# Four projections of a decoder block: output copies and search counts in program order, the forget gates beside the fifth projection

## The chip, the cores and the metric

One core of one Trainium2 chip runs the whole kernel in one launch. The metric is the device time in microseconds (us) of one execution; three executions of the kernel before took 1204.28, 1204.99 and 1205.78 us, so the time before is their median, 1204.99 us.

## The reference, cut to what matters

A decoder layer on 1024 tokens of width 1024. The input is normalised and goes through one combined projection, whose columns feed two groups of attention heads:

```python
proj = h @ w_in
(aq, ak, av, iq, ik, iw, bq, bk, bv, bf) = split(proj)
# group A: each query attends to its 256 best keys by an indexer's score
score = einsum('bqh,bqhs->bqs', iw, relu(einsum('bqhd,bsd->bqhs', iq, ik)))
_, idx = top_k(where(causal, score, -inf), 256)
# group B: a running sum of log forget gates is added to the logits
log_f = log_sigmoid(bf + b_forget)
cum = cumsum(log_f, axis=1)
logits = q @ k.T * scale + cum_q - cum_k
```

Both groups are normalised, go through an output projection, and a mixture of 32 experts follows. Nothing of that later part is touched here.

## The kernel before, in words

**Stages.** The kernel loads and normalises x, projects the indexer's keys and queries and makes the scores (`index_scores`), projects the values (`v_tile`), then projects the queries and keys of both groups, then runs sixteen attention heads as one software pipeline (n = 0 to 16), then output projection and experts. All tensors are float32; each projection is done in three passes of a high and a low part (`PASSES`), so one block of 512 output columns takes 8 x 3 = 24 matmuls (`proj_T`).

**The projection stage.** A loop over z = 0 to 3 projects queries and keys of group B, two blocks of 128 rows each (`proj_pair`, called with m = 0 and 1); after it come `KA` (keys of group A) and `QA` 0 to 3. Each call of `proj_pair` makes two halves of 512 columns. This text numbers the halves 0 to 25: z = 0 has halves 0 to 3, z = 1 has 4 to 7, z = 2 (the fifth and sixth projection) has 8 to 11, z = 3 has 12 to 15, `KA` has 16 and 17, `QA` 0 to 3 have 18 to 25. A half's result lies in one of four PSUM buffers of `ps1`, so half n can start only when the result of half n - 4 has been copied out. Two instructions copy it: `pjh` on ACT rounds it to the high part, then `pjl` on DVE subtracts that from the PSUM result for the low part. When both halves are done, two DMAs of SP store the pair to DRAM (`QB`, `KB`, `KA`, `QA`). Weights come by DMAs of SP too (`load_w`, tiles `wbr` and `waqr`); each 128 x 1024 chunk is split by ACT (high part, `wbh`, `waqh`) and POOL (low part, `wbl`, `waql`). The weights of `QA` 2 and 3 are loaded by `load_aq(1)`, which stands in program order behind `QA` 0, and SP issues its four last DMAs behind the stores of `QA` 0.

**The search.** Beside the projections the 256th best score of each query is found by bisection (`Search`, 33 steps). Each step has two groups of tiles. Group X (tiles 6 and 7) is counted by two ACT instructions (`sign`, tile `sjunk`), whose thresholds come from three small DVE instructions (`halve`, lines 492 to 494: `flag`, `low`, `low`). Group Y (tiles 5, 4, 3, 2) is counted by four DVE instructions (`tally`, 768, 640, 512 and 384 columns) and two small ones (`flip`, `bits`). Step 16 also rewrites the keys of all six tiles on DVE (`lower`). `tick(n)` emits n ticks, two of which are a step (step 16 takes four, so 68 in all): the value projections emit 12, which are steps 0 to 5, and each half of a projection emits 2 behind its copies, except the second halves of `QA` 2 and 3, which emit none; the last 8 are left for the first attention heads.

**The gates.** The forget gates of group B come from `tz`: four long DVE instructions on 8 partitions (lines 614, 617, 618, 621), a scan among them, and five on ACT (615, 616, 620, 622, 623). They depend on each other in turn: DVE `fa`, ACT exp and ln, DVE `fz` and scan, ACT `CU`, DVE `CU`, ACT `CU`. `prep(0)` reads `CU` long after, for the first attention head.

**What sets the order.** A scheduler orders the instructions of each engine by its own model of their times; each engine then runs its list strictly in that order. `ko` (`keep_in_program_order`) takes an instruction out of this choice: all instructions of an engine that have it stay in the order in which the code emits them. `paced` only keeps an instruction from being put ahead of a given matmul. Before, the copies `pjh` and `pjl` are free and the counts are paced.

Of the kernel before, what the change touches and what calls it, by code (L numbers as in the profile page):

```python
# [8 lines left out]
F32 = mybir.dt.float32  # L9
F32R = mybir.dt.float32r  # L10
# [3 lines left out]
AF = mybir.ActivationFunctionType  # L14
OP = mybir.AluOpType
# [3 lines left out]
L = 1024  # L19
# [14 lines left out]
def dap(t, off, ap):  # L34
    return bass.AP(tensor=t.tensor, offset=t.offset + off, ap=ap)
# [3 lines left out]
def hymba_block(ctx: ExitStack, tc: tile.TileContext, x, c, w_ada, b_ada, g_mix, w_in, b_forget,  # L39
# [3 lines left out]
    V, S, G, T, Q = nc.vector, nc.scalar, nc.gpsimd, nc.tensor, nc.sync  # L43
# [37 lines left out]
    def ps1(name, shape=(128, 512), dt=F32):  # L81
        return psum.tile(list(shape), dt, name=name, tag="p", bufs=4)

    def ps2(name, shape=(128, 1024), dt=F32):
        return psum.tile(list(shape), dt, name=name, tag="m", bufs=2)
# [4 lines left out]
    def dump(name, ap):  # L90
        if name in dbg:
            Q.dma_start(dbg[name], ap)
# [136 lines left out]
    p = ps2("pcol")  # L229
    for k in range(NK):  # L230
        column(p, 1, k)
    for j in range(8):
        for q in range(4 if j == 7 else 1):
            sl = slice(q * 256, (q + 1) * 256) if j == 7 else slice(0, 1024)
# [16 lines left out]
    for k in range(NK):  # L251
        hi, lo, t = u(f"hh{k}", F32R), u(f"hl{k}", F32R), u("ht")
# [27 lines left out]
    def proj_T(w, n0, n):  # L280
        p = ps1("pp")
        i = 0
        for k in range(NK):
            for a, b in PASSES:
                at["mm"] = T.matmul(p[:, :n], w(k, a), hT[b][k][:, n0:n0 + n], start=(i == 0), stop=(i == 23))  # L285
                i += 1
        return p
# [13 lines left out]
    for hf in range(2):  # L301
        sl = slice(hf * 512, (hf + 1) * 512)
        p = pk[hf]
# [64 lines left out]
    p = ps1("piw")  # L368
# [214 lines left out]
    def tick(n, mark=None):  # L583
        if mark is not None:
            at["pace"] = mark
        for _ in range(n):
            if next(steps, "end") == "end":
                return
# [3 lines left out]
    def load_b(z):  # L592
        return load_w("wb", [((C_BK if z % 2 else C_BQ) + z // 2 * 256, 256)])

    def load_aq(g):
        return load_w("waq", [(C_AQ + g * 128 + m * 64 + z * 256, 64) for m in range(2) for z in range(2)])

    def load_k():
        g2 = u("g2", shape=(128, 8, 128))
        for j in range(2):  # L600
            Q.dma_start(g2[:, j * 4:j * 4 + 4], dap(w_in, j * 512 * WIN + C_AK, [[WIN, 128], [128 * WIN, 4], [1, 128]]))
        return split(g2, "g2", (128, 8, 128), G), load_aq(0)
# [3 lines left out]
        v_tile(1, wv1, t, lambda: tick(1 + t % 2, at["mm"]))  # L606


    CU = u("CU", F32R)
    if True:  # L610
        R = slice(96, 104)
        z, a1 = u("fz"), u("fa")
        V.tensor_scalar(tz[R], tz[R], bfg[R], None, op0=OP.add)
        V.scalar_tensor_tensor(a1[R], tz[R], -1.0, tz[R], op0=OP.mult, op1=OP.max)
        S.activation(a1[R], a1[R], AF.Exp, scale=-1.0)
        S.activation(a1[R], a1[R], AF.Ln, bias=1.0)
        V.scalar_tensor_tensor(z[R], tz[R], 0.0, a1[R], op0=OP.min, op1=OP.subtract)
        V.tensor_tensor_scan(a1[R], ones[R, 0:1].to_broadcast([8, 1024]), z[R], 0.0, op0=OP.mult, op1=OP.add)
        dump("cum", a1[R])
        S.activation(CU[96:104], a1[R], AF.Copy)  # L620
        V.tensor_sub(CU[64:72], a1[R], CU[R].bitcast(F32))
        S.activation(CU[32:40], CU[R].bitcast(F32), AF.Copy, scale=-1.0)
        S.activation(CU[0:8], CU[64:72].bitcast(F32), AF.Copy, scale=-1.0)


    def proj_pair(w, cols, name, scale, beside=None):

        d = dram.tile([2, 128, L], F32, name=name)
        hi, lo = u("pjh", F32R), u("pjl", F32R)
        for hf in range(2):  # L630
            sl = slice(hf * 512, (hf + 1) * 512)
            p = proj_T(lambda k, a: w(k, a, cols), hf * 512, 512)
            S.activation(hi[:, sl], p, AF.Copy, scale=scale)
            V.scalar_tensor_tensor(lo[:, sl], p, scale, hi[:, sl].bitcast(F32), op0=OP.mult, op1=OP.subtract)  # L634
            if beside is None or not hf:
                tick(PT.pop(0), at["mm"])
            if beside:
                at["pe"] = at["pace"] = at["mm"]
                for f in beside[hf]:
                    f()  # L640
        Q.dma_start(d[0], hi.bitcast(F32))
        Q.dma_start(d[1], lo.bitcast(F32))
        return d

    QB, KB, QA = [None] * 4, [None] * 4, [None] * 4
    PT = [2] * 8 + [2] * 8 + [2] * 8
    for z in range(4):
        w, dst, g = wb, KB if z % 2 else QB, z // 2
        wb = load_b(z + 1) if z < 3 else load_k()
        for m in range(2):  # L650
            dst[g * 2 + m] = proj_pair(w, slice(m * 128, (m + 1) * 128), f"{'QK'[z % 2]}B{g}{m}", 1.0 if z % 2 else 0.125)

# [72 lines left out]
    def fill_k(par, d):  # L725
        cp(kx[par][MAIN[par]], d[0, MAIN[par]])
# [167 lines left out]
    def prep(n):  # L894
# [3 lines left out]
        if n < 8:  # L898
            h = 2 * j + par
            fill_q(par, QB[j])  # L900
            fill_k(par, KB[j])
            cp(qx[par][e + 2:e + 3], CU[96 + h:97 + h], G)
            cp(qx[par][e + 3:e + 4], CU[64 + h:65 + h], G)
            cp(kx[par][e:e + 1], CU[32 + h:33 + h], G)
# [158 lines left out]
    g2s, w = wb  # L1063
    KA = proj_pair(lambda k, a, sl: g2s[a][:, k, sl], slice(0, 128), "KA", 1.0)
    for m in range(4):
        if m == 2:
            rows, finish = max_steps(0)
            rows = [f for _, f in rows]
            beside = [rows[0:3], rows[3:5]]
        elif m == 3:  # L1070
            beside = [rows[5:7], [rows[7], finish]]
        else:
            beside = None
# [3 lines left out]
        if m == 1:  # L1077
            w = w1
            operand_tiles(0)
            prep(0)  # L1080
        if m == 2:
            operand_tiles(1)
            prep(1)
    at["pace"] = at["pe"] = at["mm"]
    after(S.preload_act_table_set("natural_log_exp_and_others"), at["mm"])

    if True:
# [342 lines left out]
    for i in range(NT):  # L1430
# [11 lines left out]
        if i in (5, 7):  # L1442
            i0, n = {5: (0, 4), 7: (4, 2)}[i]
            A, B = tables(n)
            p = count_pairs(i0, n)
# [12 lines left out]
    p = count_pairs(6, 1)  # L1458
# [10 lines left out]
    p = count_pairs(7, 1)  # L1469
# [202 lines left out]
    for e in range(NE):  # L1672
# [34 lines left out]
        else:  # L1707
            bfin = u("bfin")
            for hf in range(2):
                p = ps1("pbf")  # L1710
                for k in range(4):
                    i = 24 + hf * 4 + k
# [41 lines left out]
    with tc.If(most > 128):  # L1754
# [4 lines left out]
        f = u("ovf", shape=(128, 32, 32))  # L1759
# [30 lines left out]
        for i in range(NT):  # L1790
            for c_ in range(2):
                j = i * 2 + c_
                d = G.indirect_dma_start(
                    out=tab2d, out_offset=bass.IndirectOffsetOnAxis(ap=fi[:, 3, j:j + 1], axis=0),
                    in_=ent[:, i, c_], in_offset=None, bounds_check=NO * 128 - 1, oob_is_err=False)
# [30 lines left out]
        for o in range(NO):  # L1826
# [13 lines left out]
            for z in range(2):  # L1840
                for k in range(NK):
# [6 lines left out]
                                   op0=OP.mult, op1=OP.mult)  # L1848
# [50 lines left out]
```

## Time and profile before

| | |
|---|---|
| median of three runs | 1204.99 us |
| the profiled execution | 1199.19 us, its span 1197.2 us |
| PE busy | 1055.7 us (88%) |
| DVE busy | 919.0 us (77%) |
| ACT busy | 670.0 us (56%) |
| POOL busy | 300.3 us (25%) |

The span is the time from the first to the last instruction; 2.0 us lie around it. A row of the timeline is: start, duration, engine, line, operation, tiles, and in square brackets the idle time ahead of it and who ended that. The stage that the change touches runs from 195 to about 360 us of the span.

### The profile page before, as it was taken

To read this page: it belongs to the slowest core of one execution; us is meant where nothing else is said; L and a number is where in the kernel's file an instruction comes from. 1 tells how busy PE (TensorE), PEld (TensorE's weight loads), DVE (VectorE), ACT (ScalarE), POOL (GpSimd) and SP (SyncE) were. 2 spreads that over 40 slices of the span, in tenths; PEclk is the share of its full clock that TensorE was granted. 3 is DMA by queue.
4 is the path that set the end of the run, shared out by engine and by line. 5 is a ranking of instruction groups with operands and counts; after the bars stand their busy time and mean duration, and the time that the engine had idled before them with its cause. 6 is when DMAs were issued, how large, how long until landed. Compare 5 with 4: busy or idle time off the path is not lost.

```text
span 1197.2 us, 15378 instructions
## 1 busy us (share of the span) xinstructions
PE 1055.7 (88%) x4983; PEld 796.5 (67%) x4983; DVE 919.0 (77%) x1785; ACT 670.0 (56%) x1177; POOL 300.3 (25%) x253
## 2 busy tenths in 40 slices
PE   2789999699988998998989999975999999889881
PEld 2678899588865555654656678864777777666650
DVE  5946568899976589566578665795999999888847
ACT  7544666764546545654554622334777777656635
POOL 0341031212040110213212212551222222333223
PEclk9699999899998999999999999986999999999986
DMA  8510102243463433556336634776999999999946
GB/s 345 164 36 1 41 20 65 106 150 114 149 169 89 108 81 81 133 142 195 115 87 198 245 123 141 247 251 216 311 342 320 308 314 308 317 317 315 321 117 247
DMA packets 91414, 219.94 MB, mean 184 GB/s; under 512 B 30516, under 2 KB 40932, under 8 KB 91328
## 3 DMA queue, kind: packets, MB, share of 16 engines
q1 hardware_dynamic: 75776, 185.23, 46.5%
q0 software_dynamic: 15552, 33.66, 10.3%
q8 instruction: 42, 0.69, 0.2%
q14 instruction: 44, 0.36, 0.1%
HBM read 192.43 MB, written 42.99 MB: 197 GB/s over the span
## 4 chain that ended last, share of the span: by engine, by line
PE 49%; DVE 24%; DMA 16%; ACT 5%; issue 3%; SPq 1%; POOL 1%; DVEq 0%; ACTq 0%; POOLq 0%
PE pgu L69 10%; PE py L69 6%; PE pst L69 6%; DVE mjunk L460 6%; PE po L69 6%; PE pout L69 5%; DMA raw<-in_w_gate_dram 4%; DMA raw<-in_w_down_dram 4%; PE pp L285 3%; PE pmax L69 3%; PE pvv L407 2%; DMA qx<-mr 2%; PE pxt L74 2%; ACT sjunk L464 1%; DMA raw<-in_w_up_dram 1%
## 5 line engine op out<-in xcount | busy, mean ns | idle before, releaser
L69 PE MATMUL po<-P,VT 128*128 128x512 f32 (+3 forms) x384 | 148.3, 499 | 0.3 <-ACT P L793 0.3
L793 ACT ACTIVATE P<-pst 128x512 f32<-128x512 f32 x192 | 90.9, 489 | 95.1 <-PE pst L69 93.2
L1570 POOL DMA_INDIRECT x2d<-y,tab x31 | 59.3, 1912 | 204.9 <-DVE wgu1l L1492 46.1
L69 PE MATMUL pst<-qx,kx 128*128 128x512 f32 x192 | 94.3, 491 | 13.3 <-DMA qx<-mr 11.2
L758 DVE TENSOR_REDUCE mx<-pmax 128x1 f32<-128x128 f32 (+3 forms) x80 | 52.7, 674 | 44.6 <-PE pmax L69 44.2
L69 PE MATMUL py<-raw,af 128*128 128x512 f32 x128 | 69.2, 623 | 14.3 <-DMA raw<-in_w_down_dram 14.3
L69 PEld LDWEIGHTS po<-P,VT 128*128 128x128 f32 x384 | 66.1, 195 | 18.0 <-issue 9.8
L69 PE MATMUL pmax<-kx,qx 128*128 128x512 f32 (+1 forms) x192 | 68.1, 420 | 6.4 <-DMA kx<-KB 2.0
L69 PE MATMUL py<-wd0h,ahl 128*128 128x512 f32 x128 | 67.9, 530 | 2.4 <-ACT wd0h L1491 1.9
L69 PE MATMUL pst<-qy,ky 128*128 128x512 f32 x192 | 67.6, 352 | 0.0
L358 DVE SCALAR_TENSOR_TENSOR score<-relu,iw,score 128x384 f32<-128x384 f32 (+5 forms) x42 | 43.1, 1026 | 26.7 <-ACT relu L353 23.7
L69 PEld LDWEIGHTS pst<-qx,kx 128*128 128x128 f32 x192 | 37.9, 197 | 34.2 <-issue 20.8
L285 PE MATMUL pp<-hh,wbh 128*128 128x512 f32 x128 | 51.2, 400 | 9.3 <-DVE pjl L634 9.3
L755 DVE CUSTOM_DVE_ANT_0 mjunk<-pmax,madd 128x384 bf16<-128x384 f32 (+5 forms) x48 | 42.6, 888 | 20.6 <-PE pmax L69 20.5
L69 PE MATMUL pout<-woh,oh 128*128 128x512 f32 x128 | 52.2, 408 | 2.4 <-DVE ssq L871 2.4
L460 DVE TENSOR_SCALAR_CACHE_REDUCE mjunk<-k,low 128x768 bf16<-128x768 uint16 (+1 forms) x64 | 51.8, 810 | 1.5
L1482 POOL DMA_INDIRECT xg<-h2d,tab x32 | 39.0, 1218 | 49.6 <-PE pxt L74 35.2
L1492 DVE TENSOR_TENSOR wgu2l<-raw,wgu2h 128x512 fp32r<-128x512 f32 x64 | 43.8, 685 | 9.7 <-ACT wgu2h L1491 9.6
L285 PE MATMUL pp<-hl,wbh 128*128 128x512 f32 x128 | 50.9, 398 | 0.0
L69 PE MATMUL pout<-woh,ol 128*128 128x512 f32 x128 | 50.8, 397 | 0.0
L285 PE MATMUL pp<-hh,wbl 128*128 128x512 f32 x128 | 50.8, 397 | 0.0
L69 PE MATMUL pout<-wol,oh 128*128 128x512 f32 x128 | 50.4, 394 | 0.0
(430 smaller groups left out, 3263.1 us busy)
## 6 DMA issues: line engine op xcount, KB each, us to landing
raw<-in_w_gate_dram SPq DMA_DIRECT2D x64, 512.0 KB
raw<-in_w_up_dram SPq DMA_DIRECT2D x64, 512.0 KB
raw<-in_w_down_dram SPq DMA_DIRECT2D x64, 512.0 KB
wada<-in_w_ada_dram POOLq DMA_DIRECT2D x32, 512.0 KB, 5.5
x<-in_x_dram SPq DMA_DIRECT2D x16, 512.0 KB
wada<-in_w_ada_dram SPq DMA_DIRECT2D x16, 512.0 KB
wbr<-in_w_in_dram SPq DMA_DIRECT2D x8, 512.0 KB
qy<-QB SPq DMA_DIRECT2D x16, 256.0 KB
```

The costliest lines, as they stand in the source:

```text
L69: i = tc.keep_in_program_order(T.matmul(*a, **k))
L74: i = tc.keep_in_program_order(T.transpose(*a))
L285: at["mm"] = T.matmul(p[:, :n], w(k, a), hT[b][k][:, n0:n0 + n], start=(i == 0), stop=(i == 23))
L358: last = V.scalar_tensor_tensor(score[i], r, wv, score[i], op0=OP.mult, op1=OP.add)
L407: at["mm"] = T.matmul(p[:, :ng], hT[a][k][:, t * 128:(t + 1) * 128], parts[k // kk][b][:, k % kk, :], start=(i == 0), stop=(i == 23))
L460: paced(V.tensor_scalar(mjunk[:, :(i + 1) * 128], src, thr, None, op0=op, op1=OP.add, accum_out=self.col(self.cnt, i)))
L755: V.tensor_tensor_reduce(mjunk[:, :w_], p[:, :w_], madd[i], 1.0, NEG, OP.add, OP.max, accum_out=mx[0][:, i:i + 1])
L758: V.tensor_reduce(mx[0][:, i:i + 1], p[:, :w_], AX.X, OP.max)
L793: S.activation(P[hf, kb][0], p[:, :m], AF.Exp)
L1482: return ko(G.indirect_dma_start(out=XG[e], out_offset=None, in_=h2d, in_offset=bass.IndirectOffsetOnAxis(ap=tab[:, e:e + 1], axis=0), bou ...
L1492: ko(V.tensor_tensor(lo, w, hi.bitcast(F32), op=OP.subtract))
L1570: return G.indirect_dma_start(out=x2d, out_offset=bass.IndirectOffsetOnAxis(ap=at_, axis=0), in_=y, in_offset=None, bounds_check=L - 1, oo ...
```

## The change

Three things. The copies `pjh` and `pjl` get `ko`. While `at["pin"]` is true, from the loop over z to the end of the projections, `paced` gives `ko` to every count of the search too (and to the other paced instructions of that stretch); so the copies and the counts of an engine stand in the order of the code: copies of half n, then that half's step of the search, then the copies of half n + 1. And the gates become a function `gates()`, which is called at z = 2, between the loads for z = 3 and the fifth projection, and no longer ahead of the loop. `pinned` is defined and not used. `proj_pair` moves above the gates.

```diff
     def paced(i):
+        if at.get("pin"):
+            ko(i)
         return after(i, at["pace"]) if "pace" in at else i
...
-    CU = u("CU", F32R)
-    if True:
...
-            S.activation(hi[:, sl], p, AF.Copy, scale=scale)
-            V.scalar_tensor_tensor(lo[:, sl], p, scale, hi[:, sl].bitcast(F32), op0=OP.mult, op1=OP.subtract)
+            ko(S.activation(hi[:, sl], p, AF.Copy, scale=scale))
+            ko(V.scalar_tensor_tensor(lo[:, sl], p, scale, hi[:, sl].bitcast(F32), op0=OP.mult, op1=OP.subtract))
...
+    def gates():
+        CU = u("CU", F32R)
         R = slice(96, 104)
...
+        return CU
 
     QB, KB, QA = [None] * 4, [None] * 4, [None] * 4
+    at["pin"] = True
     PT = [2] * 8 + [2] * 8 + [2] * 8
     for z in range(4):
         w, dst, g = wb, KB if z % 2 else QB, z // 2
         wb = load_b(z + 1) if z < 3 else load_k()
+        if z == 2:
+            CU = gates()
...
     at["pace"] = at["pe"] = at["mm"]
+    at["pin"] = False
```

What stands in a row, first on ACT at the copies of halves 0 to 2 (`pjh`), before. `sjunk` is a count of the search, `wbh` a weight split, `CU` a gate instruction:

```order
L622 ACTIVATE CU<-CU 8x1024
L464 ACTIVATE sjunk,cnt_1420<-score_1026,low_1422,sga_1423 128x1024
L623 ACTIVATE CU<-CU 8x1024
L163 ACTIVATE wbh<-wbr 128x1024
L464 ACTIVATE sjunk,cnt_1420<-score_966,low_1422,sga_1423 128x896
L464 ACTIVATE sjunk,cnt_1420<-score_1026,low_1422,sga_1423 128x1024
L163 ACTIVATE wbh<-wbr 128x1024
L464 ACTIVATE sjunk,cnt_1420<-score_966,low_1422,sga_1423 128x896
L633 ACTIVATE pjh<-pp 128x512 x2
L464 ACTIVATE sjunk,cnt_1420<-score_1026,low_1422,sga_1423 128x1024
L633 ACTIVATE pjh<-pp 128x512
```

And now:

```order
L418 ACTIVATE VT_1444<-pvv 128x2x64
L418 ACTIVATE VT_1448<-pvv 128x2x64
L418 ACTIVATE VT_1450<-pvv 128x2x64
L469 ACTIVATE sjunk,cnt_1420<-score_966,low_1422,sga_1423 128x896
L168 ACTIVATE wbh<-wbr 128x1024
L469 ACTIVATE sjunk,cnt_1420<-score_1026,low_1422,sga_1423 128x1024
L621 ACTIVATE pjh<-pp 128x512
L469 ACTIVATE sjunk,cnt_1420<-score_966,low_1422,sga_1423 128x896
L469 ACTIVATE sjunk,cnt_1420<-score_1026,low_1422,sga_1423 128x1024
L621 ACTIVATE pjh<-pp 128x512
```

The first copy stood behind the gates and the counts of step 6, two copies together; now it stands behind the counts of step 5, and two counts stand between any two copies.

Second, DVE around the gates (`fz`, `fa`, `CU`), before, where counts of 768 to 384 columns (`mjunk`) stand between them:

```order
L617 SCALAR_TENSOR_TENSOR fz<-tz,fa 8x1024
L460 TENSOR_SCALAR mjunk,cnt_1433<-k_510,bits_1439 128x768
L618 SCALAR_TENSOR_TENSOR fa<-ones,fz 8x1024
L492 TENSOR_TENSOR flag_1430<-cnt_1420,need_1421 128x2
L460 TENSOR_SCALAR mjunk,cnt_1433<-k_510,bits_1439 128x640
L493 SCALAR_TENSOR_TENSOR low_1422<-flag_1430,low_1422 128x2
L460 TENSOR_SCALAR mjunk,cnt_1433<-k_510,bits_1439 128x512
L494 TENSOR_SCALAR low_1422<-low_1422 128x2
L460 TENSOR_SCALAR mjunk,cnt_1433<-k_511,bits_1439 128x384
L536 TENSOR_SCALAR flip_1441<-cnt_1433 128x4
L621 TENSOR_TENSOR CU<-fa,CU 8x1024
L538 SCALAR_TENSOR_TENSOR bits_1439<-flip_1441,bits_1439 128x4
```

And now, at half 8 (the copy `pjl` at the end is that half's):

```order
L465 TENSOR_SCALAR mjunk,cnt_1433<-k_510,bits_1439 128x512
L465 TENSOR_SCALAR mjunk,cnt_1433<-k_511,bits_1439 128x384
L639 SCALAR_TENSOR_TENSOR fa<-tz 8x1024
L541 TENSOR_SCALAR flip_1441<-cnt_1433 128x4
L543 SCALAR_TENSOR_TENSOR bits_1439<-flip_1441,bits_1439 128x4
L465 TENSOR_SCALAR mjunk,cnt_1433<-k_510,bits_1439 128x768
L465 TENSOR_SCALAR mjunk,cnt_1433<-k_510,bits_1439 128x640
L642 SCALAR_TENSOR_TENSOR fz<-tz,fa 8x1024
L643 SCALAR_TENSOR_TENSOR fa<-ones,fz 8x1024
L646 TENSOR_TENSOR CU<-fa,CU 8x1024
L622 SCALAR_TENSOR_TENSOR pjl<-pp,pjh 128x512
```

The gate instructions went from ahead of the first copy to ahead of the copy of half 8, three of them directly ahead of it.

Third, ACT at that copy, before (`wbh` is the last split for z = 3; the copies around are those of halves 6 to 9):

```order
L163 ACTIVATE wbh<-wbr 128x1024
L464 ACTIVATE sjunk,cnt_1420<-score_966,low_1422,sga_1423 128x896
L633 ACTIVATE pjh<-pp 128x512
L464 ACTIVATE sjunk,cnt_1420<-score_1026,low_1422,sga_1423 128x1024
L464 ACTIVATE sjunk,cnt_1420<-score_966,low_1422,sga_1423 128x896
L633 ACTIVATE pjh<-pp 128x512
L464 ACTIVATE sjunk,cnt_1420<-score_1026,low_1422,sga_1423 128x1024
```

And now:

```order
L469 ACTIVATE sjunk,cnt_1420<-score_1026,low_1422,sga_1423 128x1024
L168 ACTIVATE wbh<-wbr 128x1024
L640 ACTIVATE fa<-fa 8x1024
L641 ACT_TABLE_LOAD
L641 ACTIVATE fa<-fa 8x1024
L645 ACTIVATE CU<-fa 8x1024
L647 ACTIVATE CU<-CU 8x1024
L648 ACTIVATE CU<-CU 8x1024
L621 ACTIVATE pjh<-pp 128x512
L469 ACTIVATE sjunk,cnt_1420<-score_966,low_1422,sga_1423 128x896
```

Five gate instructions and a table load stand between the last split for z = 3 and the copy of half 8, where a count stood.

## Rows read from the trace of the kernel before

**Rows 1.** Windows: stretch, length, busy PE PEld DVE ACT POOL, PE clock, DMA
```profile
200.00:250.00 50.00, 40.66 (x168) 33.12 (x167) 42.87 (x123) 38.36 (x61) 9.49 (x4) 0.90 0.25 88
250.00:300.00 50.00, 49.41 (x219) 40.58 (x218) 48.07 (x127) 26.61 (x44) 12.00 (x5) 1.00 0.41 134
300.00:350.00 50.00, 47.17 (x213) 38.12 (x211) 45.55 (x130) 28.20 (x49) 16.12 (x18) 1.00 0.55 166
...
375.00:380.00 5.00, 5.00 (x21) 3.88 (x20) 0.91 (x3) 1.21 (x4) 0.00 (x0) 0.57 0.65 143
```

**Rows 2.** Waits, 150 to 420 us: in total, times, longest
```profile
PE pp L285 <- DVE pjl L634: 9.9, 2, 9.3
```

**Rows 3.** Timeline of PE: halves 0, 1, 4, 5, 16, 22, then attention
```profile
195.30 0.39 PE L285 MATMUL pp<-hh,wbh 128*128 128x512 f32 x1
...
200.78 0.39 PE L285 MATMUL pp<-hh,wbh 128*128 128x512 f32 x1
...
226.60 0.80 PE L285 MATMUL pp<-hh,wbh 128*128 128x512 f32 x1 [9.34 <-DVE pjl L634]
...
234.96 0.39 PE L285 MATMUL pp<-hh,wbh 128*128 128x512 f32 x1
...
295.55 0.50 PE L285 MATMUL pp<-hh,g2h 128*128 128x512 f32 x1 [0.59 <-DVE pjl L634]
...
332.95 0.50 PE L285 MATMUL pp<-hh,waql 128*128 128x512 f32 x1 [1.29 <-POOL waql L163]
...
373.10 0.76 PE L69 MATMUL pst<-qx,kx 128*128 128x512 f32 x1 [2.91 <-DMA qx<-mr]
```

**Rows 4.** Timeline of ACT: the gates, then the first copy
```profile
198.89 1.06 ACT L615 ACTIVATE fa<-fa 8x1024 f32<-8x1024 f32 x1 [2.08 <-DVE fa L614]
...
202.93 1.28 ACT L616 ACT_TABLE_LOAD   x1
204.22 1.05 ACT L616 ACTIVATE fa<-fa 8x1024 f32<-8x1024 f32 x1
...
210.05 1.06 ACT L620 ACTIVATE CU<-fa 8x1024 fp32r<-8x1024 f32 x1 [1.81 <-DVE fa L618]
...
225.25 1.06 ACT L633 ACTIVATE pjh<-pp 128x512 fp32r<-128x512 f32 x2
```

**Rows 5.** Timeline of DVE: the first gate, the scan, the first two copies
```profile
197.64 1.22 DVE L614 SCALAR_TENSOR_TENSOR fa<-tz 8x1024 f32<-8x1024 f32 x1
...
207.67 2.29 DVE L618 TENSOR_TENSOR_SCAN fa<-ones,fz 8x1024 f32<-8x1024 f32 x1
...
225.86 1.29 DVE L634 SCALAR_TENSOR_TENSOR pjl<-pp,pjh 128x512 fp32r<-128x512 f32 x2 [0.91 <-ACT pjh L633]
```

**Rows 6.** Timelines: counts of two successive steps on DVE; POOL's split beside DVE
```profile
237.69 1.01 DVE L460 TENSOR_SCALAR_CACHE_REDUCE mjunk<-k,bits 128x768 bf16<-128x768 bf16 x1
...
242.45 1.01 DVE L460 TENSOR_SCALAR_CACHE_REDUCE mjunk<-k,bits 128x768 bf16<-128x768 bf16 x1
...
222.34 1.69 DVE L494 TENSOR_SCALAR low<-low 128x2 f32<-128x2 f32 x1
...
221.66 2.34 POOL L163 TENSOR_TENSOR wbl<-wbr,wbh 128x1024 fp32r<-128x1024 f32 x1 [1.49 <-ACT wbh L163]
```

**Rows 7.** Timeline of DVE: step 16 begins, step 17 begins, copy of half 19
```profile
271.65 1.01 DVE L460 TENSOR_SCALAR_CACHE_REDUCE mjunk<-k,top 128x768 bf16<-128x768 bf16 x1
...
283.10 1.01 DVE L460 TENSOR_SCALAR_CACHE_REDUCE mjunk<-k,low 128x768 bf16<-128x768 uint16 x1
...
322.50 0.68 DVE L634 SCALAR_TENSOR_TENSOR pjl<-pp,pjh 128x512 fp32r<-128x512 f32 x1
```

**Rows 8.** Timelines: store of QA 0, then the split of its successor's weights
```profile
323.21 0.34 SPq L642 DMA_DIRECT2D QA<-pjl  x1
...
329.33 1.06 ACT L163 ACTIVATE waqh<-waqr 128x1024 fp32r<-128x1024 f32 x1 [0.72 <-issue]
...
330.52 2.38 POOL L163 TENSOR_TENSOR waql<-waqr,waqh 128x1024 fp32r<-128x1024 f32 x1 [5.12 <-DVE low L494]
```

More of the change, by code (lines that the diff above doesn't have):

```diff
@@ L65, in paced, with pinned @@
     def paced(i):
+        if at.get("pin"):
+            ko(i)
         return after(i, at["pace"]) if "pace" in at else i
+    def pinned(i):
+        return ko(i) if at.get("pin") else i
     def mm(*a, **k):
@@ L606, in hymba_block, with proj_pair @@
         v_tile(1, wv1, t, lambda: tick(1 + t % 2, at["mm"]))
-    CU = u("CU", F32R)
-    if True:
+    def proj_pair(w, cols, name, scale, beside=None):
+        d = dram.tile([2, 128, L], F32, name=name)
+        hi, lo = u("pjh", F32R), u("pjl", F32R)
+        for hf in range(2):
+            sl = slice(hf * 512, (hf + 1) * 512)
+            p = proj_T(lambda k, a: w(k, a, cols), hf * 512, 512)
+            ko(S.activation(hi[:, sl], p, AF.Copy, scale=scale))
+            ko(V.scalar_tensor_tensor(lo[:, sl], p, scale, hi[:, sl].bitcast(F32), op0=OP.mult, op1=OP.subtract))
+            if beside is None or not hf:
+                tick(PT.pop(0), at["mm"])
+            if beside:
+                at["pe"] = at["pace"] = at["mm"]
+                for f in beside[hf]:
+                    f()
+        Q.dma_start(d[0], hi.bitcast(F32))
+        Q.dma_start(d[1], lo.bitcast(F32))
+        return d
+    def gates():
+        CU = u("CU", F32R)
         R = slice(96, 104)
@@ L623, in hymba_block @@
         S.activation(CU[0:8], CU[64:72].bitcast(F32), AF.Copy, scale=-1.0)
[L626 to L632, printed above, removed]
-            S.activation(hi[:, sl], p, AF.Copy, scale=scale)
-            V.scalar_tensor_tensor(lo[:, sl], p, scale, hi[:, sl].bitcast(F32), op0=OP.mult, op1=OP.subtract)
[L635 to L643, printed above, removed]
+        return CU
     QB, KB, QA = [None] * 4, [None] * 4, [None] * 4
+    at["pin"] = True
     PT = [2] * 8 + [2] * 8 + [2] * 8
```

## The prediction

> **What bounds the kernel now.** I read the windows first. From 200 to 360 us PE projects, and it is the engine that sets the end there: 49.41 of 50 us busy between 250 and 300 [rows 1]. DVE is busy 48.07 in the same 50 us and 45.55 in the next [rows 1], so it hardly has room to make good a delay. Between 200 and 250 PE stands idle for 9.3 us. The waits, read next, give that to one cause: PE waits for the copy `pjl` twice in the whole stage, 9.9 us in all, and the longer one is 9.3 [rows 2]. PE's timeline then shows where: half 4 starts at 226.60 after 9.34 us, and takes until 234.96, 8.36 us, while halves 5 to 15 take (295.55 - 0.59 - 234.96) / 11 = 5.45 each [rows 3]. So the stop costs 9.34, and 2.9 more because the matmuls behind it run slowly. The two other waits are small: 0.59 at half 16, and 1.29 at half 22, for `waql` [rows 3].
>
> Why is half 4 late? The timelines of ACT and DVE show it: the first `pjh` runs at 225.25 and the first `pjl` at 225.86 [rows 4, 5], though half 0 had its matmuls done by 200.78 [rows 3]. Ahead of them stand the gates, from `fa` at 197.64 on [rows 5], and the counts between their parts.
>
> The sum below is made as a difference against the profiled execution, 1199.19 us; that lies 5.8 under the median 1204.99, and I add the difference to the median.
>
> **Half 4: the wait goes.** Up to `fa` at 197.64 [rows 5] the order is as before. Now steps 3 to 5 and then the copy follow. A step on DVE takes 242.45 - 237.69 = 4.76 us with a copy in it [rows 6], 4.1 without, so the counts end near 210. Add 1.7 for one small instruction that stands still until POOL's split is done (line 494 took 1.69, and ended with the split, 221.66 + 2.34) [rows 6], and 0.53 + 0.65 for the two copies (half of the 1.06 and 1.29 of two) [rows 4, 5]: ready near 213. PE wants half 4 at 195.30 + 4 x 5.45 = 217.1. The copy is in time by 4 us, so both the wait and the slow matmuls go: **-9.34 - 2.92 = -12.3**.
>
> **Halves 5 to 11.** The copy of half n now stands behind a whole step more for each half; a step (4.76) is shorter than a half (5.45), but POOL has four splits in such a stretch (x4 between 200 and 250) [rows 1], and each may stop DVE for 1.7. `pjl` of half 7 is then done near 213 + 7 x 4.76 + 4 x 1.7 = 253.1. PE wants half 11 at 217.1 + 7 x 5.45 = 255.2. Small waits may show; I take 0.
>
> The Trainium skill speaks against this term: "SBUF — State Buffer", section "SBUF: two separate sides", says that DVE and GpSimd share a port pair as an exclusive lock, and that the loser blocks for the whole instruction of the other. The 1.69 us of line 494 agrees with it. By that rule each split could stop DVE for up to its own 2.34, which would make 9.4 of the 6.8 and the sum 2.6 larger.
>
> **Half 12: the gates come in front of a copy.** They now stand directly ahead of `pjh` and `pjl` of half 8, which half 12 needs. Queued behind them on ACT and DVE are that copy and every later count and copy, and PE waits for these. The chain runs through both engines: `fa` 1.22, exp 1.06, table 1.28, ln 1.05, `fz` 1.22, scan 2.29, `CU` 1.06, `CU` on DVE 1.22, `CU` 1.06, then the copies 0.53 and 0.65, in sum 12.6 (the DVE instructions of `fa`'s form at its duration, the last `CU` on ACT at the first one's) [rows 4, 5]. `fa` starts near 257: half a step (2.1: three small instructions, two counts) and one more stop of 1.7 after 253.1. So `pjl` of half 8 is ready near 269.6. PE wants half 12 at 217.1 + 8 x 5.45 = 260.7; without the gates the copy would be ready near 257 + 0.53 + 0.65 = 258.2, 2.5 early. The wait is 8.9 and its matmuls run slowly as after the 9.34 before: **+8.9 + 2.9 = +11.8**. Bounds: 8.4 if two of the four stops of 1.7 don't come, 13.8 if two counts of 1.01 [rows 6] hold up the chain, as counts did before: there the first `CU` on ACT ended 13.5 after `fa` began (210.05 + 1.06 - 197.64) [rows 4, 5], where its links make 9.2.
>
> For the table load I take the row: it is 1.28 and ln starts at its end, 204.22 [rows 4]. The Trainium skill, "ScalarE: Activation LUTs", section "What ACT_TABLE_LOAD costs", adds about 1.38 us of drain to each change of set; no row here shows a drain, and with it the sum would be 1.4 larger.
>
> **Half 16.** It needs `pjl` of half 12. That of half 11 runs near 269.6 + 3 x 4.76 = 283.9. Then comes the long step 16, 283.10 - 271.65 = 11.45 [rows 7] with a copy of 0.6 in it that now stands elsewhere, and two counts of 1.01: 296.8, ready 297.5. PE wants half 16 at 269.6 + 8.36 + 3 x 5.45 = 294.3. A wait of 3.2 against 0.59 now: 0 to +2.6, and I take the middle, **+1.3** (2.9 more at the upper end, if the clock falls again).
>
> **Half 22.** `QA` 2 needs weights that SP loads behind the stores of `QA` 0, and those need the copy of half 19. That copy was done at 322.50 + 0.68 = 323.18 [rows 7]; the store followed at 323.21, the ACT split at 329.33 and POOL's at 330.52, done at 332.90 [rows 8]; PE went on at 332.95, 9.77 after the copy [rows 3]. Now the copy of half 19 stands seven steps behind that of half 12: 296.8 + 7 x 4.76 = 330.1, done 330.8, and the low weights come at 340.6. PE reaches that matmul 36.1 after half 16 starts (332.95 - 1.29 - 295.55) [rows 3], at 333.6. Wait 7.0, against 1.29: **+5.7**. On ACT the split now has a fixed place between two counts; half a step either way is 2.4, so 3.3 to 8.1. For the matmuls behind it: after the 1.29 the clock was 1.00 (300 to 350), after the 2.91 at 373.10 it was 0.57 (375 to 380) [rows 1, 3]. A wait of 7 is on that side: **+2.9**, 0 at the low end.
>
> **At no cost:** the tail of the search keeps its place in the first attention heads, and `CU` is wanted only by `prep(0)`, long after. PE's order of matmuls is unchanged.
>
> Sum: -12.3 + 11.8 + 1.3 + 5.7 + 2.9 = **+9.4**, so 1214.4 us. With all low ends -12.3 + 8.4 + 0 + 3.3 + 0 = -0.6 (1204.4), with all high ones -12.3 + 13.8 + 2.6 + 2.9 + 8.1 + 2.9 = +18.0 (1223.0).
>
> **Rivals.**
> *The gates are covered (faster).* If the copies run ahead far enough, the gates beside half 8 hide as the fifth projection's own work, and half 12 finds its buffer free. For it: the copy of half 0 would be 4 us early. Against it: the chain is 12.6 long and the margin at half 8 only 2.5. It decides at `pjl` of half 8 being ready by 260.7. Then -12.3 and 0 to +2: 1192.7 to 1194.7.
> *The wait only moves.* Half 12 loses what half 4 gains, but DVE, 0.7 a half shorter than PE (5.45 - 4.76), has made good the delay before half 19. It decides if that copy is done within 1.5 us of its place relative to half 16. Then -0.5 + 1.3 + 0 to 2: 1205.8 to 1207.8. Against it: step 16 alone takes 11.45.
> *The lag stays and every wait costs the clock (worse).* The high ends come together, at +18.0, 1223; it needs the slow matmuls at half 16 too, after a 3.2 us wait, and the 2.91 at 373.10 says that is possible.
>
> **How the numbers follow.** Forecast 0.70 (1209 to 1220), gates covered 0.10, wait only moves 0.13, worse 0.07. I take 0.2%, 2.4 us, as what a measurement of this kernel can tell from no change. Faster is the first rival, 0.10; same is the lower two thirds of the second, 0.09; the rest is slower, 0.81. The range leaves out the first rival and the upper part of the worst: 1206 to 1221.
>
> **What the changed profile would show.** If I am right: `pjl` of half 0 near 212 and no wait at half 4, near 217; the longest wait of PE for `pjl`, some 9 us, at half 12, with the gates directly ahead of that copy on ACT and DVE, and a clock below 1.00 behind it; some 3 us at half 16; some 7 us for `waql` at half 22; attention starting about 10 us later. I am wrong if `pjl` of half 8 is done before PE asks for half 12 (then the first rival), or if half 22 waits under 2 us (then the second); and by size if POOL's splits stop DVE for much more or less than four times 1.7.

## The result, and the profile after

The changed kernel takes 1217.96 us, median of five runs (1216.11 to 1219.74), against 1204.99 us for the kernel before. The ratio is 1.0104, 95% interval 1.0077 to 1.0132: slower by 12.5 us (9.3 to 15.9), where 9.4 was forecast. Its profiled execution has a span of 1216.2 us.

The windows of the changed kernel, with the columns of [rows 1]:

```profile
200.00:250.00 50.00, 50.00 (x222) 41.39 (x221) 42.55 (x121) 34.27 (x55) 12.00 (x5) 1.00 0.33 117
250.00:300.00 50.00, 32.97 (x138) 26.50 (x136) 43.05 (x83) 23.67 (x34) 10.07 (x4) 0.85 0.31 95
300.00:350.00 50.00, 44.52 (x171) 35.79 (x172) 42.67 (x140) 27.65 (x47) 10.29 (x10) 0.88 0.38 122
```

PE is now busy for all of the first 50 us, where it stood idle for 9.3 before, and for 33 of the next 50, where it was busy for 49.4. DVE is less busy there than before (43.05 against 48.07), so it isn't a greater load on DVE in this stretch that makes PE wait; what has changed is the order. The waits of PE between 150 and 420 us (total, times, longest) answer to [rows 2]:

```profile
PE pp L290 <- DVE pjl L622: 17.4, 2, 9.0
PE pp L290 <- ACT waqh L168: 3.3, 1, 3.3
...
PE pp L290 <- POOL waql L168: 1.8, 1, 1.8
```

PE's timeline places them. In order: halves 0, 4, 5, 12, 13, 16 and 17, then the two waits in half 22, and half 23:

```profile
193.87 0.39 PE L290 MATMUL pp<-hh,wbh 128*128 128x512 f32 x1
...
215.67 0.39 PE L290 MATMUL pp<-hh,wbh 128*128 128x512 f32 x1
...
221.11 0.39 PE L290 MATMUL pp<-hh,wbh 128*128 128x512 f32 x1
...
268.38 0.80 PE L290 MATMUL pp<-hh,wbh 128*128 128x512 f32 x1 [9.03 <-DVE pjl L622]
...
275.52 0.39 PE L290 MATMUL pp<-hh,wbh 128*128 128x512 f32 x1
...
300.37 0.79 PE L290 MATMUL pp<-hh,g2h 128*128 128x512 f32 x1 [8.37 <-DVE pjl L622]
...
308.48 0.39 PE L290 MATMUL pp<-hh,g2h 128*128 128x512 f32 x1
...
341.91 0.50 PE L290 MATMUL pp<-hh,waqh 128*128 128x512 f32 x1 [3.35 <-ACT waqh L168]
...
344.40 0.80 PE L290 MATMUL pp<-hh,waql 128*128 128x512 f32 x1 [1.76 <-POOL waql L168]
...
348.84 0.63 PE L290 MATMUL pp<-hh,waqh 128*128 128x512 f32 x1
```

The program reached half 0 at 193.87 here and at 195.30 before [rows 3], so every comparison below counts from half 0. The wait of half 4 is gone; half 5 starts 27.24 after half 0, where it was 39.66. Three stops have come instead: at half 12, at half 16, and twice in half 22.

**Half 12.** The gates stand ahead of the copy, as the order said. DVE's timeline (copies of halves 0, 7 and 8, the gates between them), then ACT's:

```profile
211.55 0.69 DVE L622 SCALAR_TENSOR_TENSOR pjl<-pp,pjh 128x512 fp32r<-128x512 f32 x1
...
251.91 0.68 DVE L622 SCALAR_TENSOR_TENSOR pjl<-pp,pjh 128x512 fp32r<-128x512 f32 x1
...
255.45 1.22 DVE L639 SCALAR_TENSOR_TENSOR fa<-tz 8x1024 f32<-8x1024 f32 x1
...
260.16 1.22 DVE L642 SCALAR_TENSOR_TENSOR fz<-tz,fa 8x1024 f32<-8x1024 f32 x1 [1.11 <-ACT fa L641]
261.41 2.29 DVE L643 TENSOR_TENSOR_SCAN fa<-ones,fz 8x1024 f32<-8x1024 f32 x1
264.82 1.22 DVE L646 TENSOR_TENSOR CU<-fa,CU 8x1024 fp32r<-8x1024 f32 x1 [1.12 <-ACT CU L645]
267.63 0.69 DVE L622 SCALAR_TENSOR_TENSOR pjl<-pp,pjh 128x512 fp32r<-128x512 f32 x1 [1.60 <-ACT pjh L621]
```

```profile
256.70 1.06 ACT L640 ACTIVATE fa<-fa 8x1024 f32<-8x1024 f32 x1 [5.49 <-DVE fa L639]
257.78 1.28 ACT L641 ACT_TABLE_LOAD   x1
259.07 1.05 ACT L641 ACTIVATE fa<-fa 8x1024 f32<-8x1024 f32 x1
263.73 1.05 ACT L645 ACTIVATE CU<-fa 8x1024 fp32r<-8x1024 f32 x1 [3.61 <-DVE fa L643]
...
267.03 0.57 ACT L621 ACTIVATE pjh<-pp 128x512 fp32r<-128x512 f32 x1
```

Read the two as one chain: each engine's idle time is ended by the other. From `fa` at 255.45 to the end of the copy at 268.32 it takes 12.87, and PE starts half 12 at 268.38.

**Half 16.** It needs `pjl` of half 12. DVE's timeline in step 16, then POOL's splits:

```profile
280.72 3.30 DVE L493 SCALAR_TENSOR_TENSOR k<-k,top,mjunk 128x1024 uint16<-128x1024 bf16 x1
...
290.64 2.53 DVE L492 TENSOR_SCALAR mjunk<-score,sga,sgb 128x512 uint16<-128x512 uint16 x1
293.20 2.71 DVE L493 SCALAR_TENSOR_TENSOR k<-k,top,mjunk 128x512 uint16<-128x512 bf16 x1
...
299.63 0.68 DVE L622 SCALAR_TENSOR_TENSOR pjl<-pp,pjh 128x512 fp32r<-128x512 f32 x1
```

```profile
280.12 2.82 POOL L168 TENSOR_TENSOR g2l<-g,g2h 128x1024 fp32r<-128x1024 f32 x1 [26.43 <-ACT g2h L168]
290.51 4.86 POOL L168 TENSOR_TENSOR waql<-waqr,waqh 128x1024 fp32r<-128x1024 f32 x2 [7.57 <-ACT waqh L168]
```

Three passes of step 16 (instructions of `lower`, which rewrite the keys) run beside three splits and take 3.30, 2.53 and 2.71. They end 1.1, 0.2 and 0.5 after the split that they run beside (the last two splits are a half of the 4.86 each).

**Half 22.** The copy of half 19 is at 333.85 on DVE. Then, on SP, ACT and POOL, the store of `QA` 0, the weights' loads behind it, and their split:

```profile
334.56 0.34 SPq L630 DMA_DIRECT2D QA<-pjl  x1
334.95 2.57 SPq L279 DMA_DIRECT2D waqr<-in_w_in_dram  x4
...
340.80 1.06 ACT L168 ACTIVATE waqh<-waqr 128x1024 fp32r<-128x1024 f32 x1 [7.45 <-DMA waqr<-in_w_in_dram]
...
341.98 2.36 POOL L168 TENSOR_TENSOR waql<-waqr,waqh 128x1024 fp32r<-128x1024 f32 x1 [7.24 <-ACT waqh L168]
```

### The profile page after: what moved, and what is told of

The parts are those of the page before. It is cut to its first block, busy times and chain, and to the rows that moved or that the text cites. A ratio compares the mean times of both kernels' runs of the same rounds, so it can differ in the third digit from the quotient of the medians.

```text
span 1216.2 us, 15365 instructions
## 1 busy us (share of the span) xinstructions
PE 1056.9 (87%) x4972; PEld 797.6 (66%) x4983; DVE 923.9 (76%) x1785; ACT 670.9 (55%) x1177; POOL 299.7 (25%) x253
## 4 chain that ended last, share of the span: by engine, by line
PE 49%; DVE 24%; DMA 16%; ACT 5%; issue 4%; SPq 1%; POOL 0%; DVEq 0%; ACTq 0%; POOLq 0%
PE pgu L74 10%; DVE mjunk L465 6%; PE py L74 6%; PE pout L74 5%; PE po L74 5%; PE pst L74 5%; PE pp L290 4%; DMA raw<-in_w_gate_dram 4%; DMA raw<-in_w_up_dram 3%; PE pmax L74 3%; PE pvv L412 2%; DMA qx<-mr 2%; DMA raw<-in_w_down_dram 2%; PE pxt L79 2%; DMA wada<-in_w_ada_dram 2%
## 5 line engine op out<-in xcount | busy, mean ns | idle before, releaser
L74 PE MATMUL pst<-qx,kx 128*128 128x512 f32 x192 | 94.7, 494 | 16.8 <-DMA qx<-mr 12.6
L469 ACT ACTIVATE sjunk<-score,low,sga 128x896 bf16<-128x896 uint16 (+1 forms) x34 | 40.3, 1186 | 19.4 <-DVE low L499 13.7
```

What stands on the lines that cost most here:

```text
L469: paced(S.activation(sjunk[:, :(i + 1) * 128], src, AF.Sign, bias=self.col(self.low, i), scale=scale, accum_out=self.col(self.cnt, i)))
```

## The experiments

All are compared with the kernel before, run beside them on the same chip. The table sums them up. The stage's change is the start of half 25 counted from half 0 on PE's timeline of one profiled execution, minus 155.21, which it is in the kernel before (350.51 - 195.30); the time's change is the ratio's distance from 1, times 1204.99, with its interval.

| kernel | stage, us | time, us |
|---|---|---|
| changed kernel | +13.8 | +12.5 (9.3 to 15.9) |
| e1 gates left out | +0.8 | +1.2 (-1.0 to 3.4) |
| e2 fixed order, gates as before | +7.7 | +7.4 (4.2 to 10.6) |
| e3 gates moved, order free | -0.9 | -0.8 (-3.7 to 2.0) |
| e4 fixed order, gates in pieces | +7.2 | +6.4 (3.6 to 9.0) |
| e5 weights of QA 2 loaded early | +14.6 | +15.9 (13.0 to 18.9) |
| e6 two splits on DVE | +11.5 | +14.3 (11.3 to 17.5) |
| e7 order free, pieces, 2 ticks moved | -3.9 | -5.2 (-8.3 to -1.9) |
| e8 order free, pieces, 8 ticks moved | -13.3 | -7.8 (-11.1 to -4.6) |
| e9 before, 8 ticks moved | -4.0 | +0.8 (-1.7 to 3.3) |
| e10 fixed order, pieces, 8 ticks moved | -4.3 | +2.3 (-0.1 to 4.7) |
| e11 order free, pieces, 6 ticks moved | -8.1 | -6.6 (-9.4 to -3.9) |
| e12 fixed order, gates at z = 3 | +15.0 | +15.3 (11.9 to 18.6) |

Where no counts are moved to the heads, the two columns agree within 3 us: what the change does is done by half 25.

### The change taken apart: e1 to e4, e12

**e1** leaves the gates out:

```diff
+    CU = u('CU', F32R)
+    V.memset(CU.bitcast(F32), 0.0)
     at["pin"] = True
...
-        if z == 2:
-            CU = gates()
```

> The changed kernel with the gates left out (CU is set to zero ahead of the loop over z), the fixed order of copies and counts kept. Theory (the gates in front of the copy of half 8 cost their whole chain, and the fixed order makes the later waits by itself): the 9.0 us wait at half 12 and its 1.7 us of slow matmuls go, a wait of some 6 to 9 us at half 16 and some 5 us for the weights at half 22 stay, so about 10.7 under the changed kernel, near 1207. Rival (the fixed order alone makes DVE late, the gates are covered): half 12 still waits over 5 us, and the time stays within 4 us of 1218.

1207.07 us. Half 12 no longer waits, half 16 waits 6.2, half 22 3.3 and 1.8, as the theory had it. Leaving the gates out is worth 11.3 us. That isn't yet the price of their place, since their own work, 5.95 us on DVE (three times 1.22 and the scan's 2.29), is gone too; e2 tells the two apart. PE's half 16:

```profile
289.25 0.79 PE L290 MATMUL pp<-hh,g2h 128*128 128x512 f32 x1 [6.21 <-DVE pjl L622]
```

**e2** keeps the order and puts the gates back:

```diff
+    CU = gates()
     at["pin"] = True
...
-        if z == 2:
-            CU = gates()
```

> The fixed order kept, the gates back ahead of the loop over z. Theory: the copy of half 0 stands two counts behind the last gate on DVE (213.9 in the kernel before), so near 216, in time for half 4 at 217; half 4 waits 0 to 2 us, halves 5 to 12 under 1.5 each, half 16 some 6 to 9, half 22 some 5, in sum 3 to 8 us over the kernel before, 1208 to 1213. Rival (the place of the gates is the whole loss): the half-4 wait goes and nothing takes its place, 1193 to 1196.

1213.15 us, 7.4 over the kernel before. Half 4 waits 2.71 in place of 9.34, halves 11 and 12 0.62 and 0.77, half 16 8.32, half 22 3.78 and 1.73. The rival falls: with the gates where they were, the fixed order takes most of half 4's wait away and gives all of it back, and more, at half 16 and half 22. By the ratios some 6 of e1's 11.3 us (7.4 - 1.2) are the gates' own work, and some 5 (12.5 - 7.4) the price of their new place in a fixed order, both give or take some 4; the stage's change has 6.9 and 6.1.

**e3** moves the gates and fixes nothing (no `ko` on copies, `at["pin"]` not set).

> The gates moved beside the fifth projection, copies and counts free for the scheduler as before. Theory (the gates need not cost 11 us there, since counts and copies can go between their links, and the free order keeps the weights of half 22 in time): no wait at half 4, some 4 us at half 12, 2 to 5 at half 16, under 1.5 at half 22, in sum 2 to 6 under the kernel before, 1199 to 1203. Rival (the new place costs its chain in any order): half 12 waits 9 again, 1210 or more.

1206.78 us, no change to be told. The waits are about as expected (5.64 at half 12, 4.60 at half 16, none at half 22), but the time forecast is missed: half 12 took 7.28 and half 16 8.34 in place of 5.44, which the sum of the waits had left out. The gates' place alone costs nothing and brings nothing in the time, though it takes half 4's wait away without any fixed order.

**e4** cuts the gates into seven pieces, each fixed behind the step of one of halves 4 to 10:

```diff
                 tick(PT.pop(0), at["mm"])
+            if next(nh) in (4, 5, 6, 7, 8, 9, 10):
+                next(gate)
...
+        ko(V.scalar_tensor_tensor(ga[R], tz[R], -1.0, tz[R], op0=OP.mult, op1=OP.max))
+        yield
+        ko(S.activation(ga[R], ga[R], AF.Exp, scale=-1.0))
+        ko(S.activation(ga[R], ga[R], AF.Ln, bias=1.0))
+        yield
...
```

> The fixed order kept, the gates cut into seven pieces in a fixed place each, one behind the step of each of halves 4 to 10, so that no copy has the whole chain ahead of it. Theory: half 12 waits under 3 us in place of 9.0, half 16 some 8 to 11 (the DVE work is the same, and PE comes earlier), half 22 some 5; 5 to 8 under the changed kernel, 1210 to 1213. Rival (DVE is simply full, and the chain does not matter): the waits only change places, 1216 to 1220.

1214.15 us: half 12 waits 2.13, half 16 9.23, half 22 3.54 and 1.77. By its ratio this is 6.1 us under the changed kernel. Counted from half 0, half 13 starts 7.9 earlier than in the changed kernel and half 17 6.7 earlier. The whole chain ahead of one copy cost these 7.9; the stops at half 16 and half 22 stay.

Two counts from half 0 tell the order's own part. The copy of half 12 ends at 100.1 in the kernel before, 100.6 in e2, 99.4 in e3 and 99.8 in e4: with all of DVE's work in the stage it comes then, in a fixed order and in a free one, and half 16 gives back what half 4 gained. It ends at 106.4 in the changed kernel, where the whole chain stands ahead of a copy, and at 93.6 in e1, without the gates. So the stop at half 16 is not the order's own. The one at half 22 is, in these runs: from half 22 to half 24 the changed kernel, e1, e2 and e4 lose 6.7 to 6.9 us against the kernel before, and e3 gains 1.6.

**e12** calls the gates four halves later (`if z == 3`).

> The changed kernel with the gates called at z = 3 in place of z = 2, four halves later, the order fixed as in it. Theory (the wait follows the gates): half 12 waits under 2 us in place of 9.0, and half 16 some 14 to 18, the sum of the gates' chain and of step 16; half 22 some 5 to 7; within 4 us of the changed kernel, 1214 to 1222. Rival (the wait at half 12 is the fixed order's, not the gates'): half 12 still waits over 5.

1221.85 us. Half 12 doesn't wait, and half 16 waits for the gates' chain and for step 16 together, more than was expected:

```profile
303.94 0.79 PE L290 MATMUL pp<-hh,g2h 128*128 128x512 f32 x1 [19.72 <-DVE pjl L622]
```

### The later two stops: e5 and e6

**e5** calls the loads of the weights of `QA` 2 and 3 ahead of `QA` 0:

```diff
+    w1 = load_aq(1)
     for m in range(4):
...
-        if m == 0:
-            w1 = load_aq(1)
```

> The changed kernel with one edit: the loads of the weights of QA 2 and 3 are called ahead of QA 0, so SP no longer issues the last four of them behind the stores of QA 0 and the copy of half 19. Theory (half 22 waits 3.35 and 1.76 because these loads stand behind that store): both waits and the slow matmuls behind them go, PE's halves 22 to 24 come about 6 us earlier, and at least half of that stays to the end, 1211 to 1215. Rival (the first attention head waits for something that the copies and the counts set on DVE, so the time at half 22 is given back there): half 24 starts 6 earlier and the heads do not, within 2.4 us of the changed kernel. The waits at half 12 (9.0) and half 16 (8.4) stay by both.

1220.76 us; the theory falls, and the rival holds. Half 22 no longer waits, and half 24 starts 151.06 after half 0, where it was 161.07 (354.94 - 193.87). Then all of it is lost. DVE's copy of half 21, SP behind it, and the first head on PE:

```profile
350.36 0.68 DVE L622 SCALAR_TENSOR_TENSOR pjl<-pp,pjh 128x512 fp32r<-128x512 f32 x1
```

```profile
351.07 0.33 SPq L630 DMA_DIRECT2D QA<-pjl  x1
351.49 0.60 SPq L727 DMA_DIRECT2D qx<-qx  x1
```

```profile
354.09 0.45 PE L74 MATMUL pmax<-kx,qx 128*128 128x128 f32 x1 [6.18 <-DMA qx<-qx]
```

The small copy `qx<-qx`, which completes the first head's operand, now stands on SP behind the store of `QA` 1, and that store waits for the copy of half 21, which ends at 351.04. In the changed kernel SP issues it ahead of the stores of `QA` 1, and what holds it there is POOL, which clears `qx` only behind the late split:

```profile
345.38 0.59 SPq L727 DMA_DIRECT2D qx<-qx  x1
```

So the early load took one holder of the first head away, and the new order on SP put another in its place, through which the delay of DVE's copies reaches the head. What the early load brings with `qx<-qx` ahead of that store was not run.

**e6** lets DVE make the two low parts `waql` that POOL made during step 16 (`load_w` gets the engine; `split(..., eng or G, pin)`, with V for the first load).

> The changed kernel with one edit: the low parts of the first QA weights (two splits, 4.86 us on POOL, during step 16) are made by DVE; the split of KA's weights stays on POOL as a control. Theory (DVE's small passes of step 16 stand still while POOL splits): the two passes of 512 columns (2.53 and 2.71 us) fall to 0.55 and 0.75, the pass of 1024 columns beside KA's split stays near 3.3; DVE pays about 1.2 for each split itself, so half 16 waits 1 to 3 us less than 8.37, and the time falls by 0 to 3 us, near 1216. Rival (these passes are long for another reason, their data or the ACT work beside): their durations stay.

The passes of 512 columns fall to 0.55 and 0.75, and the pass beside KA's split, which stays on POOL, keeps its 3.30; half 16 waits 5.83 in place of 8.37:

```profile
280.39 3.30 DVE L493 SCALAR_TENSOR_TENSOR k<-k,top,mjunk 128x1024 uint16<-128x1024 bf16 x1
...
290.30 0.55 DVE L492 TENSOR_SCALAR mjunk<-score,sga,sgb 128x512 uint16<-128x512 uint16 x1
290.88 0.75 DVE L493 SCALAR_TENSOR_TENSOR k<-k,top,mjunk 128x512 uint16<-128x512 bf16 x1
...
292.79 1.22 DVE L168 TENSOR_TENSOR waql<-waqr,waqh 128x1024 fp32r<-128x1024 f32 x1
```

So it is POOL's split that stops these passes. The stage is some 2 us shorter for it. The time doesn't show that: 1218.46 us, with a ratio of 1.0119 (1.0094 to 1.0145), can't be told from the changed kernel's 1.0104.

### Versions meant to beat both: e7 to e11

**e7, e8 and e11** drop `at["pin"]`, keep the copies in their order and the gates in pieces, and take counts out of the stage: two ticks (one step) from halves 11 and 12, eight from halves 8 to 15, six from halves 6 to 11. The attention heads do them, in e8 and e11 with four ticks a head. Of e8:

```diff
-    at["pin"] = True
-    PT = [2] * 8 + [2] * 8 + [2] * 8
+    PT = [2] * 8 + [1] * 8 + [2] * 8
...
-            r += spread([lambda: tick(1, at["pe"])] * (3, 3, 3, 3)[n], 0, 0.9)
+            r += spread([lambda: tick(1, at["pe"])] * (4, 4, 4, 4)[n], 0, 0.9)
```

> An attempt to beat both: counts free again, the copies in their order, the gates in seven pieces, one each behind the steps of halves 4 to 10, and one count step (two ticks) moved from halves 11 and 12 to the first attention heads. Theory (DVE is full in the stage: only work taken out of it, and a chain that stands ahead of no copy, lets PE keep the 12 us of half 4): no wait at halves 4 and 12, 5 to 9 us with slow matmuls at half 16, under 1.5 at half 22; 3 to 8 under the kernel before, 1199 to 1204. Rival (the step that was moved costs as much in the heads): within 2.4 of the kernel before.

> As the run with two ticks moved, but eight ticks (four steps) moved from halves 8 to 15 to the attention heads, which take four ticks each. Theory: no wait for a copy in the whole projection stage, the clock stays up, the heads start 15 us earlier; part of it is given back in heads 0 to 4, whose DVE now has four more steps of some 4.8 us; 4 to 9 under the kernel before, 1198 to 1203. Rival (the heads are bound by DVE, and the four steps cost 19 us there): slower than the kernel before by 3 or more.

> The free order with the gates in pieces, and six ticks (three steps) moved from halves 6 to 11 to the heads. Theory: no wait at halves 4, 12 and 16, some 2 us at half 22, and a step less in the heads than with eight ticks: 0.5 to 0.8% under the kernel before, as the run with eight within 3 us. Rival (eight was already more than the stage can use, so every step that stays in it is free): 2 or more under the run with eight.

1200.26, 1198.41 and 1198.03 us, with ratios to the kernel before of 0.9957 (0.9931 to 0.9984), 0.9935 (0.9908 to 0.9962) and 0.9945 (0.9922 to 0.9968): all three beat both kernels, and the intervals don't tell e8 from e11. In e7 half 16 still waits 8.38, in a free order. In e11 halves 12 and 16 don't wait, but half 22 waits 0.39, 2.70 and 1.75, more than was expected. In e8 no half waits for a copy, and half 22 waits 1.66 for `waql`; its windows:

```profile
200.00:250.00 50.00, 50.00 (x222) 41.43 (x221) 43.98 (x132) 37.20 (x61) 9.61 (x4) 1.00 0.29 103
250.00:300.00 50.00, 49.88 (x220) 40.95 (x219) 42.08 (x96) 24.69 (x38) 13.31 (x5) 1.00 0.46 150
300.00:350.00 50.00, 45.62 (x213) 35.42 (x212) 44.27 (x117) 25.45 (x44) 16.06 (x18) 1.00 0.64 180
```

The clock is 1.00 throughout and the stage ends 13.3 earlier; 5.5 of it is lost again by the end. The heads now do eight ticks more, and e9 and e10, with the same eight, lose 4.8 and 6.6 behind the stage too.

**e9** moves the same eight ticks in the kernel before, and **e10** in the fixed order with the pieces.

> The kernel before with one edit: eight ticks (four steps) of the search moved from halves 8 to 15 to the attention heads, which take four each; gates and order as before. Theory (the gain of the runs with pieces needs both: the gates away from the first copy and DVE work out of the stage): half 4 still waits 9.3, nothing else in the stage waited over 1.3, so the move only costs in the heads, 0 to 6 over the kernel before. Rival (moving the counts alone makes the gain): 4 or more under it.

> The fixed order with the gates in pieces, and eight ticks moved from halves 8 to 15 to the heads: as the free run with eight, but copies and counts fixed. Theory (the fixed order does harm because DVE is full, and its waits at half 16 go once four steps are out; the weights of half 22 stay late, since the split stands between fixed counts): half 12 waits under 3, half 16 under 2, half 22 some 5; 4 to 10 over the free run with eight, about the kernel before, 1202 to 1209. Rival (a fixed order costs by itself, in halves 4 to 16 too): 1212 or more.

e9: 1206.73 us, no change. Half 4 waits 9.33 as before: moving counts alone pays nothing. e10: 1208.69 us, ratio 1.0019 (0.9999 to 1.0039). Its halves 12 and 16 wait 1.35 and 0.16, but half 22 waits 4.97 and 1.27; it stands 10 us over e8, which differs from it only in that the counts are free. With room on DVE the fixed order no longer delays the copies that halves 12 and 16 need. But the copy of half 19 ends 11.3 after half 20 has started, against 6.6 in e8, and with it the weights of half 22 come late. A fixed order isn't the only way to that: in e11, whose counts are free, that copy ends 9.6 after the start of half 20.

## Why the prediction was right, and where its sum was off

The direction, the time (1214.4 forecast, 1217.96 measured) and the places of the three stops were right. That the time came so near is in part luck: half 16 came out 9.0 above its term, and half 12, half 22 (at half 24) and half 25 came out 0.9, 1.8 and 1.8 below theirs. The terms, each from the starts of the next half counted from half 0, in both kernels:

| term | forecast | measured |
|---|---|---|
| half 4 | -12.3 | -12.4 |
| halves 5 to 11 | 0 | 0 |
| half 12 | +11.8 | +10.9 |
| half 16 | +1.3 | +10.3 |
| half 22 | +8.6 | +6.1 at half 23, +6.8 at half 24 |
| half 25 | 0 | -1.8 |

- **Half 4 and the copies up to half 7.** The copy of half 0 is at 211.55 and ends 18.4 after half 0; 17.7 was forecast. From there to the copy of half 7 it takes 40.36, forecast 40.1 with four stops of 1.7 behind POOL's splits. This match is luck: the trace has three stops in that stretch, and 2.00 of waiting for a count on ACT. DVE's first stop, and the split beside it:

```profile
225.68 2.15 DVE L541 TENSOR_SCALAR flip<-cnt 128x4 int32<-128x4 f32 x1
```

```profile
225.40 2.40 POOL L168 TENSOR_TENSOR wbl<-wbr,wbh 128x1024 fp32r<-128x1024 f32 x1 [15.84 <-ACT wbh L168]
```

The three take 2.15, 1.16 and 2.10 in place of 0.15 to 0.17, so 4.9 us were lost and not 6.8. The Trainium skill, "SBUF — State Buffer", section "SBUF: two separate sides", would have let each cost up to a whole split; the trace agrees as far as each of the three stood until its split ended, and lost about what was left of the 2.40, 1.0 to 2.0.
- **Half 12.** The chain took 12.87 from `fa` to the copy, forecast 12.6. The wait is 9.03 (8.9), but the slow matmuls cost 1.7 (275.52 - 268.38 - 5.44), not 2.9. e12 shows that the wait goes where the gates go. The term is half 12's alone: by e2 their new place costs some 5 to 6 us in the end. The Trainium skill, "ScalarE: Activation LUTs", section "What ACT_TABLE_LOAD costs", would add a drain of about 1.38 us: ln starts at 259.07, where the load that began at 257.78 ends, so the trace shows none.
- **Half 16 is the step that failed.** I took step 16 at its length in the kernel before, 11.45, and forecast a wait of 3.2 and a term of 1.3. The wait was 8.37, and its slow matmuls cost 2.7 more (308.48 - 300.37 - 5.44). Counted from half 0, PE wanted half 16 at 98.1 (forecast 99.0), and the copy was ready at 106.4 (forecast 102.2): nearly all of the miss is 4.2 us on DVE. POOL's splits of `g2` and `waqr` fell into step 16's passes; that stopped DVE for 6.0 us (3.30, 2.53 and 2.71 against the 1.28 of the same pass in the kernel before, and e6's 0.55 and 0.75), where the 11.45 held one stop of 1.7, a pass of 2.35 that takes 0.68 now. In e2, e4 and e12 three of these passes are stopped too, in e3 and e7, with free counts, one each. e6 takes two of them away, and the wait falls by 2.5. The half 16 that waits and drops the clock was in my third rival; the middle of 0 and 2.6 was the wrong choice.
- **Half 22.** From the end of the copy of half 19 to the end of `waql` it took 9.8 (344.34 - 334.54), forecast 9.77. The term was nearly right in size. That it can be had back by itself is not shown: e5 takes both waits away and gains nothing, because in its order on SP the first head's operand stands behind a late copy. e10 against e8 speaks for a cost of its own: between half 22 and half 24 e10 loses 7.4 us more, and in the time 10.
- **At no cost:** borne out; the first heads show two new small waits (1.72 and 0.77, for `P` on ACT), none for the search or for `CU`. The -1.8 at half 25 is for the most part a wait of the kernel before, 1.54 for `kx<-CU` at the first head, that is covered now.
- The rivals: "the gates are covered" fell with half 12's 9.03. "The wait only moves" fell by its own sign: the copy of half 19 ends 34.2 after half 16 starts (334.54 - 300.37), where it was 27.6, so DVE has not made good the delay. Its core held in another place: by the copy of half 12 in e2, e3 and e4, what half 4 gains goes at half 16.

The two profiled executions differ by 19.0 us in span, though half 0 came 1.4 earlier. From half 0 to half 25 it is 13.8; the other 6.6 come later, in stages whose instructions are the same in both; the runs of one kernel differ by as much (the kernel before, beside e1 to e4: 1197.0 to 1214.1), so I don't explain it.

## What to carry to other kernels

An order fixed by hand brings a late copy forward, but whatever has it on an engine waits in that order: look for the chain that goes to and fro between two engines, and keep it from standing whole ahead of something that a third engine waits for. A stall that is taken away comes back at the next place where the buffers run out, unless work is also taken off the engine that makes the copies; here neither the gates' move (e3) nor fewer counts (e9) paid alone, and both together, with the gates in pieces, gave 0.43 to 0.65%. Before counting on a wait, ask what its removal puts in its place: in e5 loads moved ahead also moved a small copy behind a late store, and all was lost again.

## What was not expected of the hardware

A wait of PE costs more than its length, and not in proportion: in the half behind it, waits of 1.35, 2.13 and 2.71 us (e10, e4, e2) cost 0.1 to 0.2 us over 5.44, those of 4.60, 8.37, 9.03 and 9.34 cost 2.9, 2.7, 1.7 and 2.9, and all fifteen from 4.60 to 19.72 cost 1.5 to 2.9. The windows behind half 16's wait in the changed kernel (PE clock is the third number from the end):

```profile
300.00:304.00 4.00, 3.63 (x9) 2.85 (x10) 3.79 (x13) 2.86 (x5) 0.00 (x0) 0.50 0.12 47
304.00:308.00 4.00, 4.00 (x15) 3.23 (x14) 3.79 (x15) 2.25 (x4) 0.00 (x0) 0.77 0.21 84
308.00:312.00 4.00, 4.00 (x19) 3.31 (x18) 3.82 (x13) 2.03 (x6) 0.00 (x0) 1.00 0.33 131
```

The clock is at its lower level, 1.2 GHz, when PE starts again, and at the full 2.4 GHz 8 us later. And some instructions of DVE stood still until POOL's split ended, the passes of step 16 and the small `flip` and `flag` among them, while others did not: the copy `pjl` at 251.91, which reads PSUM, ran in its usual 0.68 beside a split from 251.30 on, and in the kernel before two counts took 0.75 and 0.60, as elsewhere, beside a split from 253.43 to 255.85.
